# Two projected tiles of a Mamba-2 stage accumulate in another PSUM pool

## The chip, the cores and the metric

The kernel runs on 1 core of one Trainium2 chip. The metric is the device time of one launch in microseconds (us), the median of several runs. TensorE (PE) multiplies matrices into PSUM, VectorE (DVE), ScalarE (ACT) and GpSimd (POOL) work elementwise, and SyncE (SP) issues most of the DMAs. Each engine takes its instructions strictly in the order in which they were built and waits at the first one whose operands are not ready.

## The reference

One inference step of a two-layer trunk for 256 prompt tokens and 8 x 8 sample tokens, 320 columns together. Layer 0 mixes with a chunked gMLP, layer 1 with a Mamba-2 SSD block, and each is followed by a squared-ReLU MLP. The change is in the SSD block:

```python
def mamba2_mixer(h, ...):
    zxbcdt = h @ w_in                      # 1024 -> 2048 z, 4096 xbc, 32 dt
    xbc_c = silu(conv(xbc))                # causal, width 4
    dt = softplus(dt_raw + dt_bias)
    y, new_ssm = ssd_scan(xs, dt, -exp(a_log), bm, cm, ssm_state)
    y = (y + xs * d_skip) * silu(z)
    out = rms_norm(y by group, norm_g) @ w_out
```

Here `ssd_scan` needs the running sum of `dt * a` over the positions (`acum`), its exponentials, the products C B^T per group, and per head small products with the state. There are 8 groups of 4 heads.

## The kernel before

Activations lie transposed, features on the 128 partitions and the 320 columns in the free dimension. A weight matrix is read in tiles of 1024 x 128. Each is loaded by a DMA on SP's queue into `raw` (5 buffers), rounded on ACT to `whi` (L136) and its remainder taken on DVE as `wlo` (L137), with 3 buffers each (`NHI`). A tile then takes 8 x 3 matmuls of 128 x 320 (L307, L308, L309: `whi` with the high and the low part of the input, `wlo` with the high part), which accumulate in one PSUM bank.

PSUM has four pools. `psm` (names `mm`) has three banks and `psx` (names `ax`) three; `psa` (`adap`) and `psn` (`nrm`) have one each. Projected tiles take a bank of `mm`. The small products of the SSD work take banks of `ax`.

In the SSD stage the first five tiles (`w_dt` and `w_in` 0 to 3) are computed ahead of the norm. From index 4 on `in_tile` calls `proj_h`, one tile at a time. The order of the tiles, by their index i, is by groups of six: B, C, two of X, two of Z. Group 1 has i = 6 to 11, so i = 8 and 9 (the ninth and the tenth) are its two X tiles, and 10 and 11 its two Z tiles. B, C and X go through `conv` (L634): an evacuation by ACT into `cb` (three buffers, L640 and L641), a convolution of one ACT and three DVE instructions (L646, L649), and a SiLU (L651, L652). A Z tile is read by one ACT instruction (L815).

Beside the tiles runs a chain for `dt` (L820 to L860): a series on DVE (L829), the scan for `acum` (L836), exponentials on ACT (L838), the packing on POOL (L845 to L848), two stores to DRAM (L850, L851), and PE transposes of the packed rows (L854, L859). From the stored rows each group loads `bc` and `ea`, broadcast to all partitions (L673, L674); `bc` has two buffers. The convolutions after the first ones are held back behind the scan (L647).

`ssd` does one group's work in pieces (`yield`), which `convs` of the next group interleaves with its tiles: C B^T into `pc` (L681) and its masking to `cbm` on DVE (L683); the decay factors in `bc` by twelve ACT instructions (L687) and an exponential (L688); transposes (L697 to L717); state products (L735); `cp` (L745); the outputs (L757); the gating with Z (POOL L769), squares (ACT L774) and their mean (DVE L776, PE L210); the new state (L785 to L802).

The order on each engine isn't that of the code. The tile framework is opened with `schedule_with_timeline_sim=True`: it simulates the whole program with its own estimates of durations, and places each instruction on its engine, and each tile in a buffer of its pool, by that timeline. A change in one place can so move instructions on every engine behind it. `tc.issue_after` adds a constraint to that order.

Of the kernel before, what the change touches and what calls it, by code (L numbers as in the profile page):

```python
# [52 lines left out]
def tile_trunk(ctx: ExitStack, tc: tile.TileContext, io):  # L53
    nc = tc.nc
    pe, act, dve, pool = nc.tensor, nc.scalar, nc.vector, nc.gpsimd
# [12 lines left out]
    def nm(s):  # L68
        uid[0] += 1
        return f"{s}{uid[0]}"  # L70
# [30 lines left out]
    def mm_ps():  # L101
        return psm.tile([P, 512], F32, tag="mm", name=nm("mm"))

    def ax_ps():
        return psx.tile([P, 512], F32, tag="ax", name=nm("ax"))
# [34 lines left out]
    def wload(src, w=P, eng=dve):  # L140
        fill["n"] += fill["rate"]
        while fill["n"] >= 1:
            fill["n"] -= 1
            if fill["q"]:
                step()
        raw = raw_tile()
        nc.sync.dma_start(raw, src)
        return [t.rearrange("p (a b) -> p a b", b=w) for t in split(raw, eng=eng)]
# [156 lines left out]
    def mm3(ps, w, kk, hi, lo, first, last, n=T):  # L305
        whi, wlo = w
        pe.matmul(ps[:, :n], lhsT=whi[:, kk, :], rhs=hi, start=first, stop=False)  # L307
        pe.matmul(ps[:, :n], lhsT=whi[:, kk, :], rhs=lo, start=False, stop=False)  # L308
        pe.matmul(ps[:, :n], lhsT=wlo[:, kk, :], rhs=hi, start=False, stop=last)  # L309

    def proj1(srcs, hi, lo, eng=dve):
        ps = mm_ps()
        n = 8 * len(srcs)
        for kc, src in enumerate(srcs):
            w = wload(src, eng=eng)
            for kk in range(8):
                k = kc * 8 + kk
                mm3(ps, w, kk, hi(k), lo(k), k == 0, k == n - 1)
        return ps

    h_hi = lambda k: hhi[:, k, :]
    h_lo = lambda k: hlo[:, k, :]

    def proj_h(src, eng=dve):
        return proj1([src], h_hi, h_lo, eng)

    def proj_g(src, g, ps):
        ghi, glo, _ = g
# [5 lines left out]
    def scaled(ps, r):  # L334
        c = tp.tile([P, 10], F32, tag="sc", name=nm("sc"))
        act.copy(c, ps[:, T:G])
        t = scratch()
        dve.tensor_tensor(t, ps[:, :T], r, MUL)
        dve.tensor_tensor(b1(t[:, TP:]), b1(t[:, TP:]), bb(c[:, 1:9]), ADD)
        dve.tensor_scalar(t[:, :TP], t[:, :TP], c[:, 0:1], None, ADD)  # L340
        return t
# [5 lines left out]
    def mlp(l, gc, g, nxt):  # L347
        A, S = amul[2 * l + 1], mod(l, 3)
        r = rstd_x()
        c, mp = new_pool("left" if l else "right")  # L350
        mhi = mp.tile([P, NF, T], F32R, name=f"mhi{l}")
        mlo = mp.tile([P, NF, T], F32R, name=f"mlo{l}")

        def ev1(m, ps):
            t = scratch()
            act.activation(t, ps[:, :T], AF.Relu)  # L356
            s = scratch()
            pool.tensor_tensor(s, t, t, MUL)  # L358
            act.activation(mhi[:, m, :], s, AF.Copy)  # L359
            dve.tensor_tensor(mlo[:, m, :], s, mhi[:, m, :].bitcast(F32), SUB)  # L360

        pss = [proj_g(io["mlp_w1"][l, m], g, mm_ps() if m < 3 else ax_ps()) for m in range(MG)]
        gc.close()
        ev1(0, scaled(pss[0], r))
        norm(A, S, r)
        for m in range(1, MG):
            ev1(m, scaled(pss[m], r))
        for m in range(MG, NF):
            ev1(m, proj_h(io["mlp_w1"][l, m]))
        ng = nxt()  # L370
        gate = mod(l, 5)
        for m in range(KD):
            ps = proj1([io["mlp_w2"][l, m, kc] for kc in range(4)], lambda k: mhi[:, k, :], lambda k: mlo[:, k, :])
            residual(ps, m, gate, ng)
        c.close()
        return ng
# [191 lines left out]
    for m in range(16):  # L568
        ev_u(m, proj_h(io["gm_wu"][m]))
        while len(us) > 9:  # L570
            spatial(sp)
            sp += 1
# [9 lines left out]
    for m in range(KD):  # L582
        ps = proj1([io["gm_wo"][m, kc] for kc in range(2)], lambda k: uhi[:, k, :], lambda k: ulo[:, k, :])
        residual(ps, m, gate, g)
# [35 lines left out]
    ps = scaled(pss[0], r0)  # L620
# [6 lines left out]
    def in_tile():  # L627
        i = widx[0]
        widx[0] += 1
        if i < MG - 1:  # L630
            return scaled(pss[1 + i], r0)
        return proj_h(io["w_in"][i])

    def conv(ct, tag, bufs):  # L634
        ps = in_tile()
        cb = mb.tile([P, CW], F32, tag="cb", name=nm("cb"), bufs=3)
        cs = cb[:, 3 + TP :].rearrange("p (b t) -> p b t", t=11)
        pool.memset(cb[:, 0:3], 0.0)
        pool.tensor_copy(cs[:, :, 0:3], scv[:, ct])
        act.copy(cb[:, 3 : 3 + TP], ps[:, :TP])  # L640
        act.copy(cs[:, :, 3:], b1(ps[:, TP:T]))  # L641
        pool.tensor_copy(cvp[:, ct, :], cb[:, TP : TP + 3])
        pool.tensor_copy(scv[:, ct], cs[:, :, 8:])
        o = mb.tile([P, CW], F32, tag="co", name=nm("co"), bufs=3)
        wv = lambda k: vec[:, V_CW + ct * 4 + k : V_CW + ct * 4 + k + 1]
        act.activation(o[:, :CO], cb[:, :CO], AF.Identity, scale=wv(0), bias=vec[:, V_CB + ct : V_CB + ct + 1])  # L646
        with tc.issue_after(dtl[0]) if dtl else ExitStack():  # L647
            for k in range(1, 4):
                dve.scalar_tensor_tensor(o[:, :CO], cb[:, k : k + CO], wv(k), o[:, :CO], MUL, ADD)  # L649
        r = mb.tile([P, T], F32, tag=tag, name=nm(tag), bufs=bufs)  # L650
        act.activation(r[:, :TP], o[:, :TP], AF.Silu)  # L651
        act.activation(b1(r[:, TP:]), o[:, 3 + TP :].rearrange("p (b t) -> p b t", t=11)[:, :, 0:8], AF.Silu)  # L652
        return r
# [150 lines left out]
    def convs(g_, prev):  # L804
        B = conv(16 + g_, "Bt", 2)
        next(prev, None)
        C = conv(24 + g_, "Ct", 2)
        next(prev, None)
        X = []
        for r in range(2):  # L810
            X.append(conv(2 * g_ + r, "Xt", 4))
            next(prev, None)
        Z = mt([P, 2, T], "Z", 2)
        for r in range(2):
            act.activation(Z[:, r], in_tile()[:, :T], AF.Silu)  # L815
            next(prev, None)
        return B, C, X, Z
# [291 lines left out]
```

## Time and profile before

| | us |
|---|---|
| median of 3 runs | 1078.03 |
| lowest, highest | 1077.81, 1082.76 |
| the profiled execution | 1075.66 |
| its span, first to last instruction | 1073.9 |
| PE busy in the span | 1030.2 (96%) |
| DVE, ACT, POOL busy | 652.9, 549.2, 299.9 |

The span lies 1.8 us below the execution's own time, for what is ahead of the first instruction and behind the last. PE is busy nearly all the time, and its clock is granted at one of two levels, 1.2 or 2.4 GHz. In the page's row of clocks a 9 is (nearly) all of a slice at 2.4 GHz; the share over the span is 0.986. The SSD stage with its 48 projected tiles stands between about 500 and 760 us.

### The profile page before, as it was taken

Reading aid. Unit: us, or ns where it says so; the run is one execution under the profiler, and the core shown is the slowest. Engines: PE = TensorE matmul, PEld = TensorE weight load, DVE = VectorE, ACT = ScalarE, POOL = GpSimd, SP = SyncE. Lnnn points to the kernel's source line nnn. Section 1 sums busy time; section 2 is a strip of 40 time slices with the busy share of each in tenths; the row PEclk is TensorE's granted clock in tenths of the full one; section 3 lists DMA queues with packets and bytes.
Section 4 is the critical chain, followed back from the end, with each engine's and each line's share of the span. In section 5 each row is a group of like instructions: output and inputs, shape, how many; then the busy total and the mean of one; then the engine's idle time right before and its main releaser. Section 6 shows DMA issues by size and latency. Waiting matters only on the chain.

```text
span 1073.9 us, 19747 instructions
## 1 busy us (share of the span) xinstructions
PE 1030.2 (96%) x7809; PEld 970.8 (90%) x7809; DVE 652.9 (61%) x1080; ACT 549.2 (51%) x1013; POOL 299.9 (28%) x403
## 2 busy tenths in 40 slices
PE   5999999999999999999688999999999999999996
PEld 3778998999999999999688999999999999999995
DVE  4545966437644443446968898898876754444432
ACT  4453343435644433335698777678345555543331
POOL 1200134332433311222123333532217243411001
PEclk9999999999999999999888999999999999999998
DMA  9957985775666667455435656565445544544431
GB/s 366 361 194 237 335 316 166 267 253 195 243 215 216 217 223 271 151 157 172 151 108 171 251 168 222 197 224 205 167 163 158 177 157 140 155 153 144 155 99 50
DMA packets 60877, 213.97 MB, mean 199 GB/s; under 512 B 6560, under 2 KB 12128, under 8 KB 58480
## 3 DMA queue, kind: packets, MB, share of 16 engines
q1 hardware_dynamic: 58544, 200.47, 55.1%
q0 software_dynamic: 1952, 11.98, 3.1%
q8 instruction: 61, 1.00, 0.4%
q10 hardware_dynamic: 288, 0.26, 0.1%
q14 instruction: 32, 0.26, 0.1%
HBM read 199.31 MB, written 12.85 MB: 198 GB/s over the span
## 4 chain that ended last, share of the span: by engine, by line
PE 76%; ACT 7%; DVE 6%; issue 5%; DMA 3%; POOL 2%; SPq 0%; POOLq 0%; ACTq 0%; DVEq 0%
PE mm L307 19%; PE mm L308 19%; PE mm L309 19%; PE adap L165 3%; ACT bc L687 2%; DMA bc<-rowd 2%; DVE wlo L137 2%; DVE co L649 2%; ACT whi L136 1%; PE mm L411 1%; PE mm L412 1%; PE mm L413 1%; PE ax L757 1%; DMA raw<-ada 1%; PE ax L307 1%
## 5 line engine op out<-in xcount | busy, mean ns | idle before, releaser
L137 DVE TENSOR_TENSOR wlo<-raw,whi 128x1024 fp32r<-128x1024 f32 (+1 forms) x243 | 298.1, 1228 | 203.5 <-ACT whi L136 202.6
L136 ACT ACTIVATE whi<-raw 128x1024 fp32r<-128x1024 f32 (+1 forms) x243 | 254.7, 1050 | 252.4 <-PE mm L308 195.0
L307 PE MATMUL mm<-hhi,whi 128*128 128x320 f32 x952 | 300.1, 316 | 1.9 <-ACT ta L356 0.9
L308 PE MATMUL mm<-hlo,whi 128*128 128x320 f32 x952 | 296.8, 313 | 0.1
L309 PE MATMUL mm<-hhi,wlo 128*128 128x320 f32 x952 | 296.9, 313 | 0.0
L307 PEld LDWEIGHTS mm<-hhi,whi 128*128 128x128 f32 x952 | 180.2, 190 | 7.5 <-issue 3.3
L308 PEld LDWEIGHTS mm<-hlo,whi 128*128 128x128 f32 x952 | 180.1, 189 | 1.9 <-DVE hlo L267 1.0
L309 PEld LDWEIGHTS mm<-hhi,wlo 128*128 128x128 f32 x952 | 180.0, 189 | 1.4 <-DVE mv L198 0.4
L307 PE MATMUL mm<-mhi,whi 128*128 128x320 f32 x512 | 158.3, 309 | 0.0
L308 PE MATMUL mm<-mlo,whi 128*128 128x320 f32 x512 | 158.1, 309 | 0.0
L309 PE MATMUL mm<-mhi,wlo 128*128 128x320 f32 x512 | 158.0, 309 | 0.0
L358 POOL TENSOR_TENSOR ta<-ta 128x320 f32<-128x320 f32 x64 | 82.0, 1285 | 140.0 <-ACT ta L356 118.2
L307 PEld LDWEIGHTS mm<-mhi,whi 128*128 128x128 f32 x512 | 96.1, 188 | 1.2 <-issue 0.8
L308 PEld LDWEIGHTS mm<-mlo,whi 128*128 128x128 f32 x512 | 96.1, 188 | 0.0
L309 PEld LDWEIGHTS mm<-mhi,wlo 128*128 128x128 f32 x512 | 96.1, 188 | 0.0
L293 POOL TENSOR_TENSOR x<-x,rs 128x64 f32<-128x64 f32 x28 | 11.2, 399 | 218.5 <-DVE rs L292 218.5
L359 ACT ACTIVATE mhi<-ta 128x320 fp32r<-128x320 f32 x64 | 30.1, 471 | 81.9 <-POOL ta L358 81.6
L360 DVE TENSOR_TENSOR mlo<-ta,mhi 128x320 fp32r<-128x320 f32 x64 | 33.5, 523 | 59.2 <-ACT mhi L359 59.2
L649 DVE SCALAR_TENSOR_TENSOR co<-cb,vec,co 128x344 f32<-128x344 f32 x96 | 54.7, 585 | 6.1 <-ACT co L646 5.9
L165 PE MATMUL adap<-ara,sc 128*32 128x256 f32 x640 | 43.0, 383 | 0.0
L307 PE MATMUL mm<-uhi,whi 128*128 128x320 f32 x128 | 40.0, 315 | 0.0
L308 PE MATMUL mm<-ulo,whi 128*128 128x320 f32 x128 | 40.0, 315 | 0.0
(340 smaller groups left out, 1691.8 us busy)
## 6 DMA issues: line engine op xcount, KB each, us to landing
raw<-mlp_w SPq DMA_DIRECT2D x128, 512.0 KB, 3.6
ara<-ada_w SPq DMA_DIRECT2D x80, 512.0 KB, 6.3
raw<-w_in SPq DMA_DIRECT2D x48, 512.0 KB, 3.7
raw<-ada SPq DMA_DIRECT2D x16, 512.0 KB, 9.9
raw<-gm_wv SPq DMA_DIRECT2D x16, 512.0 KB, 8.7
raw<-gm_wu SPq DMA_DIRECT2D x16, 512.0 KB, 5.8
raw<-gm_wo SPq DMA_DIRECT2D x16, 512.0 KB, 5.3
st<-state SPq DMA_DIRECT2D x8, 1024.0 KB, 5.5
```

The source lines that it names most:

```text
L136: act.activation(hi[:, :n], raw[:, :n], AF.Copy)
L137: eng.tensor_tensor(lo[:, :n], raw[:, :n], hi[:, :n].bitcast(F32), SUB)
L165: pe.matmul(ps[32 * j : 32 * j + 32, :256], lhsT=sc[:, kb + i, :], rhs=rs[i][:, j * 256 : (j + 1) * 256], start=(kb + i == AB - 1), stop=( ...
L293: (dve if m == KD - 1 else pool).tensor_tensor(x[:, m, TP:], x[:, m, TP:], t0, ADD)
L307: pe.matmul(ps[:, :n], lhsT=whi[:, kk, :], rhs=hi, start=first, stop=False)
L308: pe.matmul(ps[:, :n], lhsT=whi[:, kk, :], rhs=lo, start=False, stop=False)
L309: pe.matmul(ps[:, :n], lhsT=wlo[:, kk, :], rhs=hi, start=False, stop=last)
L358: pool.tensor_tensor(s, t, t, MUL)
L359: act.activation(mhi[:, m, :], s, AF.Copy)
L360: dve.tensor_tensor(mlo[:, m, :], s, mhi[:, m, :].bitcast(F32), SUB)
L649: dve.scalar_tensor_tensor(o[:, :CO], cb[:, k : k + CO], wv(k), o[:, :CO], MUL, ADD)
L687: act.activation(bc[:, h, cq[c]], bc[:, h, cq[c]], AF.Relu, bias=nat[:, c, HG * g_ + h : HG * g_ + h + 1], scale=-1.0)
```

## The change

`proj1` and `proj_h` take an optional PSUM tile. `in_tile` passes a bank of `ax` for i = 8 and i = 9; all other tiles keep `mm`.

```diff
-    def proj1(srcs, hi, lo, eng=dve):
-        ps = mm_ps()
+    def proj1(srcs, hi, lo, eng=dve, ps=None):
+        ps = ps or mm_ps()
...
-    def proj_h(src, eng=dve):
-        return proj1([src], h_hi, h_lo, eng)
+    def proj_h(src, eng=dve, ps=None):
+        return proj1([src], h_hi, h_lo, eng, ps)
...
         if i < MG - 1:
             return scaled(pss[1 + i], r0)
-        return proj_h(io["w_in"][i])
+        return proj_h(io["w_in"][i], ps=ax_ps() if i in (8, 9) else None)
```

No instruction is added or removed in the computation. The order changes on all engines from about 521 us on. In the rows below the tiles' accumulators are, by i: `mm870` 7, `mm883` or `ax883` 8, `mm897` or `ax897` 9, `mm909` 10, `mm916` 11, `mm931` 12; `whi` and `wlo` with numbers near theirs are their weights.

PE at the head of the stage, before: tile 8 ends, then come the packed rows' transposes, group 0's first products, and tile 9.

```order
L309 MATMUL mm883_5629<-hhi_81,wlo886_5633 128x320
L854 MATMUL ax823_5329<-cst_78,yst1_5250 128x128 x3
L859 MATMUL ax825_5336<-cst_78,dup0824_5334 128x128 x2
L697 MATMUL adap880_5619<-cst_78,Bt833_5364 128x128 x2
L681 MATMUL ax868_5547<-Ct838_5385,Bt833_5364 128x128 x2
L681 MATMUL ax868_5547<-Ct838_5385,Bt833_5364 128x64
L307 MATMUL mm897_5698<-hhi_81,whi899_5701 128x320
```

PE at the same place of the changed kernel:

```order
L309 MATMUL mm916_5842<-hhi_81,wlo919_5846 128x320
L854 MATMUL ax823_5329<-cst_78,yst1_5250 128x128 x3
L859 MATMUL ax825_5336<-cst_78,dup0824_5334 128x128 x2
L697 MATMUL adap880_5619<-cst_78,Bt833_5364 128x128 x2
L681 MATMUL ax868_5547<-Ct838_5385,Bt833_5364 128x128 x2
L681 MATMUL ax868_5547<-Ct838_5385,Bt833_5364 128x64
L307 MATMUL mm931_5923<-hhi_81,whi933_5926 128x320
L308 MATMUL mm931_5923<-hlo_82,whi933_5926 128x320
L307 MATMUL ax883_5629<-hhi_81,whi885_5632 128x320
```

Tiles 10 and 11 have moved ahead of the transposes, and tile 8 behind them and behind the first two matmuls of tile 12. Tiles 8 and 9 are given the same bank of `ax`, the one that `pc` (`ax868`) holds before; tiles 10 and 11 share one bank of `mm`, while tiles 6 and 7 hold the other two.

DVE shortly behind that place, the difference (- before, + now): the masking of `pc`, the product `cp` that needs the loaded `ea`, and convolutions.

```order
 L649 SCALAR_TENSOR_TENSOR co842_5401<-cb841_5394,vec_79,co842_5401 128x344
-L683 TENSOR_TENSOR cbm869_5551<-ax868_5547,cst_78 128x320
 L745 TENSOR_TENSOR cp907_5753<-ea828_5343,Ct838_5385 128x768
 L649 SCALAR_TENSOR_TENSOR co847_5422<-cb846_5415,vec_79,co847_5422 128x344
 L649 SCALAR_TENSOR_TENSOR co866_5539<-cb865_5532,vec_79,co866_5539 128x344
 L649 SCALAR_TENSOR_TENSOR co847_5422<-cb846_5415,vec_79,co847_5422 128x344
+L683 TENSOR_TENSOR cbm869_5551<-ax868_5547,cst_78 128x320
```

The masking, which frees the bank of `pc`, has moved behind `cp` and three convolution steps.

ACT some 160 us later, while tile 35 is projected and group 4's output is finished: the squares (L774) of group 4 and the decay factors (L687) on the `bc` that is loaded for group 6.

```order
 L613 COPY dup21229_7727<-Xt1183_7429 128x256
-L774 ACTIVATE Z1118_7021<-Y1193_7476 128x640
 L687 ACTIVATE bc1209_7607<-bc1209_7607,nat_5087 128x128 x2
 L687 ACTIVATE bc1209_7607<-bc1209_7607,nat_5087 128x64
 L687 ACTIVATE bc1209_7607<-bc1209_7607,nat_5087 128x128 x2
 L687 ACTIVATE bc1209_7607<-bc1209_7607,nat_5087 128x64
-L687 ACTIVATE bc1209_7607<-bc1209_7607,nat_5087 128x128
-L136 ACTIVATE whi1235_7742<-raw1234_7740 128x1024
-L687 ACTIVATE bc1209_7607<-bc1209_7607,nat_5087 128x128
-L815 ACTIVATE Z1188_7443<-mm1196_7530 128x320
+L687 ACTIVATE bc1209_7607<-bc1209_7607,nat_5087 128x128 x2
+L774 ACTIVATE Z1118_7021<-Y1193_7476 128x640
```

The squares have moved from ahead of the first decay factors to behind eight of the twelve. On PE there, the mean (L210 into `nrm1201`) stood behind 24 matmuls of tile 35 and 19 of tile 36 after the outputs of group 4; now it stands behind 20 and 11.

## Rows read from the trace of the kernel before

**Rows 1.** The page: span, granted clock by slice, and the weight remainders' group.

```profile
span 1073.9 us, 19747 instructions
...
PEclk9999999999999999999888999999999999999998
...
L137 DVE TENSOR_TENSOR wlo<-raw,whi 128x1024 fp32r<-128x1024 f32 (+1 forms) x243 | 298.1, 1228 | 203.5 <-ACT whi L136 202.6
```

**Rows 2.** PE's waits: line and releaser, us in total, times, longest.

```profile
PE ax L854 <- POOL yst L847: 8.1, 1, 8.1
PE ax L794 <- DVE xst L729: 2.9, 1, 2.9
...
PE ax L735 <- ACT Bn L701: 1.8, 1, 1.8
...
PE adap L713 <- DVE Bst L704: 1.3, 2, 1.0
...
PE nrm L210 <- DVE ta L776: 0.6, 1, 0.6
```

**Rows 3.** Three stretches: PE, PEld, DVE, ACT, POOL busy (instructions), granted clock, DMA.

```profile
531.27:544.92 13.65, 7.50 (x29) 6.70 (x30) 10.20 (x19) 9.85 (x32) 5.22 (x16) 0.50 0.63 199
544.92:568.82 23.90, 19.25 (x203) 18.45 (x203) 15.99 (x26) 23.79 (x53) 4.26 (x18) 1.00 0.29 93
568.82:575.64 6.82, 6.82 (x25) 5.71 (x23) 6.82 (x6) 6.24 (x19) 3.54 (x2) 0.50 0.48 148
```

**Rows 4.** PE in order of time at the stage's head: start, us, [idle before <-releaser].

```profile
520.59 0.31 PE L307 MATMUL mm<-hhi,whi 128*128 128x320 f32 x1
...
522.24 0.31 PE L307 MATMUL mm<-hhi,whi 128*128 128x320 f32 x1
...
524.00 0.31 PE L307 MATMUL mm<-hhi,whi 128*128 128x320 f32 x1
...
536.37 0.90 PE L854 MATMUL ax<-cst,yst 128*128 128x128 f32 x3 [8.10 <-POOL yst L847]
...
540.75 0.61 PE L307 MATMUL mm<-hhi,whi 128*128 128x320 f32 x1
...
546.01 0.38 PE L699 MATMUL adap<-cst,dup 128*128 128x128 f32 x2
```

**Rows 5.** ACT, then DVE, in order of time at the same place.

```profile
524.93 1.06 ACT L136 ACTIVATE whi<-raw 128x1024 fp32r<-128x1024 f32 x1 [1.63 <-PE mm L308]
...
524.48 2.07 DVE L829 SCALAR_TENSOR_TENSOR yst<-yst 128x320 f32<-128x320 f32 x4
...
532.22 0.95 DVE L836 TENSOR_TENSOR_SCAN yst<-cst,yst 128x320 f32<-128x320 f32 x1
...
542.50 0.96 DVE L745 TENSOR_TENSOR cp<-ea,Ct 128x768 f32<-128x768 f32 x1 [0.99 <-DMA ea<-rowd]
543.38 3.01 DVE L649 SCALAR_TENSOR_TENSOR co<-cb,vec,co 128x344 f32<-128x344 f32 x6
```

**Rows 6.** PE, SP, ACT and DVE in order of time behind group 4's outputs.

```profile
687.39 0.41 PE L307 MATMUL mm<-hhi,whi 128*128 128x320 f32 x1
...
688.86 0.38 SPq L673 DMA_DIRECT2D bc<-rowd  x1
...
693.86 0.74 ACT L774 ACTIVATE Z<-Y 128x640 f32<-128x640 f32 x1 [5.55 <-POOL Y L769]
...
694.64 0.49 DVE L776 TENSOR_TENSOR ta<-Z 128x320 f32<-128x320 f32 x1 [2.23 <-ACT Z L774]
...
695.05 2.05 ACT L687 ACTIVATE bc<-bc,nat 128x128 f32<-128x128 f32 x7 [0.45 <-DMA bc<-rowd]
...
695.18 0.83 PE L210 MATMUL nrm<-ones_g,ta 128*128 128x1 f32 x6 [0.58 <-DVE ta L776]
```

**Rows 7.** The loads of `bc` (line 673): who waited (us, times), and landing.

```profile
  ACT bc L687: 15.0, 5
...
DMA to landing us min/median/max: 4.1/5.2/6.5
```

## Prediction

> **What bounds the kernel now.** I read the page first: PE fills the span but for small gaps, and the granted clock sags in three slices at the SSD stage and in the last one [rows 1]. So time can be won or lost only as idle time of PE or as time at 1.2 GHz. PE's waits, read next, name one big idle, 8.1 us at the transposes of the packed `dt` rows (L854), and behind it 2.9 us at the new state (L794) and 1.8 us at L735; the rest of the stage has waits of about 1 us and less [rows 2]. The busy time by stretch then shows what the clock adds: 1.2 GHz from 531.27 to 544.92, behind the first idle, and again for 6.82 us from 568.82, right behind the wait at L794, while between them it was full; 0.50 in that view is 1.2 GHz and 1.00 is 2.4 [rows 3]. All three views point at the head of the stage, which is where the change begins; the timelines of PE, ACT and DVE there show why [rows 4, 5]. PE stops at 528.27 (536.37 less 8.10) because the two accumulators of group 1's B and C tiles cannot be emptied until group 0's convolutions go on, and those are held behind the scan, which starts at 532.22.
>
> A matmul of a tile costs 0.147 us at 2.4 GHz: 12 of them from 522.24 to 524.00 [rows 4], so a tile of 24 costs 3.53. At 1.2 GHz it is about 0.27: 25 in 6.82 us [rows 3]. A stretch of 6.82 us at the low clock therefore loses 6.82 x (1 - 0.147/0.27) = 3.1 us.
>
> The profiled execution took 1075.66 us, its span and 1.8 us around it; the median of the three runs is 2.37 us higher. I work out the difference against the profiled execution and put it on the median of 1078.03.
>
> **The change part by part.** No instruction is added or taken away, so the sum is one of waits. I take three places.
>
> *First place, 520 to 546 us.* The two tiles that leave `mm` let tiles 10 and 11 (Z, whose accumulator one SiLU empties without the held convolution) run ahead of L854. That is one tile more, 3.53 us of work, in front of the wait of 8.10. But these two do not run freely.
>
> Tile 7 starts at 520.59 and ends by 24 x 0.147 at 524.1. The weights of tiles 8 and 9 are already cast and keep two of the three `whi` buffers until those tiles run, now behind L854. So the cast for tile 10 waits for tile 7's last use of the third, and takes 1.06 [rows 5]: tile 10 starts at about 525.3. Its third matmul needs `wlo`, which stands on DVE behind three steps of the series (four take 2.07) and takes 1.23 [rows 1, 5]: about 527.2. With 22 x 0.147 it ends at 530.5. The same third buffer serves tile 11: cast until 531.6, then the SiLU of tile 10 must empty their common bank, and tile 11 starts at about 531.9. Its `wlo` stands on DVE behind the scan and three convolution steps of 0.50 [rows 5]: one remainder fewer than before stands ahead of the scan, so this ends at 532.2 + 0.95 - 1.2 + 1.5 = 533.5, and the remainder at 534.7. Then 22 matmuls at 0.147 or 0.27: tile 11 ends, and L854 starts, between 538.0 and 540.7. Before, it started at 536.37.
>
> Behind L854, tile 8 waits for the bank of `pc`, that is for `cbm`, and on DVE `cbm` now stands behind `cp`, which waits for the `ea` load. That load hangs on ACT's exponential of the scan. The scan is earlier, but ACT has the SiLU of tile 10 and a table load ahead of the exponential, so I leave the arrival at 542.50 as it is [rows 5]. `cp` 0.96, three steps of 0.50 and `cbm` 0.49: tile 8 starts at about 545.5, with 2 matmuls of tile 12 done. Before, tile 9 started at 540.75 and by 546.01 had 21 of its 24 matmuls [rows 4]. At 546 the old order so has tiles 7, 8 and 21 matmuls; the new one has 7, 10, 11 and 2 to 5 matmuls of 12 and 8, 5 to 8 ahead, 0.7 to 1.2 us. Whether the clock stays low a little longer is open by about 2 us. I take 0 for this place, from -2 to +2. The idle of 8.10 isn't removed; it is cut into waits for casts, for one bank and for a mask.
>
> *Second place, 546 to 687 us.* Group 0's outputs (L757) stood behind 2 matmuls of tile 13 and now stand behind all of it and 2 each of tiles 14 and 15. Two tiles of cover come in front of L735 and L794, so their 1.8 and 2.9 go, and with them probably the low clock behind L794: 1.8 + 2.9 + 3.1 = 7.8 us won at most. What is late next: the groups' chains run two tiles later against the projections for groups 0 and 1, one for group 2. The `bc` loads, which wait for the outputs of two groups before, come later by as much, and five of the eight hold ACT up already, 15.0 us in all [rows 7]; casts stand behind them. Tiles 13, 14 and 15 start in turn with two matmuls each, and each needs a cast and a remainder of 1.06 + 1.23 in which PE has 0.3 us of work: 2 us or so are lost there. At L713, which waits for `Bst` on DVE, the longest wait was 1.0; two remainders stand near it now, so 1 to 2.5 us in one group. A few waits of the 1 us kind follow from the shift, and one more stretch of low clock (3.1) is as likely as not. That is 5 to 10 us against 7.8. I take 0, from -6 to +4.
>
> *Third place, 687 to 702 us.* Times are from the first matmul behind group 4's outputs, 687.39. Before, PE reached L210 at 695.18 - 0.58 = 694.60, after 43 matmuls and eight of L794: 7.21 us. Now 31 stand ahead: 7.21 - 12 x 0.147 = 5.45. The release came at 7.79. From PE's order alone the wait grows from 0.58 to 2.34. But ACT's squares now stand behind eight decay factors on a `bc` that is still in flight: issued at 688.86, in use at 695.05, which is 7.66. Eight of L687 at 2.05 / 7 = 0.29 give 10.0, the squares 0.74, DVE's sum 0.49 and the two hand-overs 0.1: 11.3. The wait is then 11.3 - 5.45 = 5.9, 5.3 more than before. `bc` took 6.1 here; with the shortest and the longest of the eight loads (4.1 and 6.5) [rows 6, 7] the growth is 3.3 and 5.7. Both idles of 2.9 us and more in this stage were followed by the low clock and those of 1.8 and less were not [rows 2, 3], so I add 3.1, with 0 as the other end. Together +8.4, from +3.3 to +8.8.
>
> The Trainium skill speaks against this change in the same direction ("TensorE: Matmul & The Clock Gate", section "HAM oscillation — how this bites in real kernels"): a stream of matmuls that is cut again and again by waits falls back to the half clock each time and pays for the way back each time, so several middling waits can cost more than one long one. The trace agrees where it can, with the 3.1 us behind a wait of only 2.9. By that rule the sum is the one taken here; without it, it is 3.1 less.
>
> Sum: 0 + 0 + 8.4 = +8.4, which I round to +8. On the profiled execution that is 1083.7, on the median **1086**.
>
> **The rivals.**
>
> *The wait at L854 goes and nothing takes its place (faster).* One tile more runs in front of it, and the low clock behind it is shorter. For it: 8.10 idle and 13.65 us at low clock are the largest loss in the span. Against it: only 3.53 us of work is added, and the casts of both tiles are chained through one buffer. Worth at most 3.5 of idle, 2 of clock at the head, and the 7.8 of the second place; less 4 at a mild third place that is 9: 1078 - 9 = 1069. It decides if casts and masks come about 2 us earlier than I have them.
>
> *The new order loses as much as it wins (no change).* If `bc` lands in 4.1 us at the third place and the clock holds there, it costs 3.3, and 2 to 3 won at the second place cancel it: 1078 to 1080. For it: the loads' spread of 4.1 to 6.5. Against it: the order on ACT is fixed, so some of the 5 us is lost in every case.
>
> *More places like the third (slower still).* The same order, decay factors ahead of other work, can hold ACT in other groups, and each wait near 3 us can bring 3.1 of low clock. With two more, +14: 1092. For it: the 15.0 us that ACT waits for `bc` already. Against it: by group 4 the outputs stand at nearly their old place again, so the shift dies out.
>
> *The tiles do not get another bank of use.* Tile 8 in `ax` waits for `pc`, and the pool gives no spare bank; in effect the change only swaps the Z tiles with the X tiles. This is already in the sum.
>
> **How the numbers follow.** Forecast, +8 with its own range of 1081 to 1090: 0.56. Slower still: 0.18. No change: 0.18. Faster: 0.08. About 0.5%, 5.4 us, is what a measurement of this kernel can tell from no change: 1072.6 to 1083.4. Of the forecast's case a small part lies below 1083.4, about as much as of the no-change case lies above. So faster 0.08, same 0.18, slower 0.74. The range 1078 to 1093 leaves out the faster case, the low half of no change and the far end of the slower one.
>
> **What would show it.** In the profile after, PE's wait at L854 should be gone or under 1 us, with waits of 1 to 2 us at L307 and L309 for `whi` and `wlo` just ahead of it, and one of about 2 us at the start of the tile in `ax`, released by DVE L683. The waits at L794 and L735 near 552 and 568 should be gone. A wait of 4 to 6 us at L210 released by DVE L776, some 10 us later in the span than before, should be the largest of the stage, with the clock at 1.2 GHz behind it. If L210's wait stays under 2 us, or the kernel comes out under 1075, the third place is wrong; if PE idles nowhere and the time is still longer, the whole sum is.

## The result and the profile after

The changed kernel took 1089.76 us (median of 20 runs, 1084.11 to 1096.18), the kernel before 1078.78 in the same rounds (20 runs, 1075.36 to 1084.54): a ratio of **1.0095, with a 95% interval of 1.0077 to 1.0113**. The change makes the kernel slower by about 1%. The profiled execution of the changed kernel took 1084.21 us, 8.55 more than that of before, and it is one of the quickest of its runs; what follows explains these 8.55 us, and of the other 2.4 by which the medians differ only the runs' times speak.

The page after, its span and the granted clock by slice (before: [rows 1]):

```profile
span 1082.4 us, 19739 instructions
...
PEclk9999999999999999999999999899999999999998
```

The page counts 8 instructions fewer than before; PE, DVE and POOL compute with as many as before, and ACT has two loads of its function tables (ACT_TABLE_LOAD) less. The three slices of 8 at the head of the SSD stage (some 510 to 590 us) are gone. One slice of 8 has come far behind them, from 676 to 704 us: it is the third place. PE's waits from 500 us on (line and releaser, us in total, times, longest; before: [rows 2]):

```profile
PE nrm L210 <- DVE ta L776: 6.0, 2, 4.9
PE mm L307 <- ACT whi L136: 4.5, 4, 1.8
PE mm L307 <- ACT Z L815: 4.2, 2, 2.9
PE mm L309 <- DVE wlo L137: 3.7, 2, 2.4
...
PE ax L307 <- DVE cbm L683: 1.1, 1, 1.1
...
PE adap L713 <- DVE Bst L704: 0.3, 1, 0.3
```

The waits of 8.1 at L854, 1.8 at L735 and 2.9 at L794 are gone (of L794 a wait of 0.2 is left, with another releaser). In their place stand casts (`whi`, `wlo`), a SiLU (`Z`, L815), a mask (`cbm`), and 4.9 us at L210. To see where each is, the head first, PE in order of time (start, us, idle before and its releaser; before: [rows 4]):

```profile
525.94 0.42 PE L307 MATMUL mm<-hhi,whi 128*128 128x320 f32 x1 [1.00 <-ACT whi L136]
...
527.87 0.41 PE L309 MATMUL mm<-hhi,wlo 128*128 128x320 f32 x1 [1.38 <-DVE wlo L137]
...
532.69 0.41 PE L307 MATMUL mm<-hhi,whi 128*128 128x320 f32 x1 [1.33 <-ACT Z L815]
...
535.60 0.42 PE L309 MATMUL mm<-hhi,wlo 128*128 128x320 f32 x1 [2.35 <-DVE wlo L137]
...
540.47 0.49 PE L854 MATMUL ax<-cst,yst 128*128 128x128 f32 x3
...
543.78 0.42 PE L307 MATMUL mm<-hhi,whi 128*128 128x320 f32 x1 [1.77 <-ACT whi L136]
...
545.42 0.41 PE L307 MATMUL ax<-hhi,whi 128*128 128x320 f32 x1 [1.08 <-DVE cbm L683]
```

L854 follows its neighbour without a gap, at 540.47 instead of 536.37: a tile more lies in front of it, and so do four waits of 6.06 us together. Then the third place, in rows of PE, SP, ACT and DVE (before: [rows 6]):

```profile
686.90 0.41 PE L308 MATMUL mm<-hlo,whi 128*128 128x320 f32 x1
...
687.98 0.38 SPq L673 DMA_DIRECT2D bc<-rowd  x1
...
693.71 2.33 ACT L687 ACTIVATE bc<-bc,nat 128x128 f32<-128x128 f32 x8 [6.28 <-DMA bc<-rowd]
695.96 0.72 ACT L774 ACTIVATE Z<-Y 128x640 f32<-128x640 f32 x1
...
696.71 0.49 DVE L776 TENSOR_TENSOR ta<-Z 128x320 f32<-128x320 f32 x1 [5.19 <-ACT Z L774]
...
697.25 1.44 PE L210 MATMUL nrm<-ones_g,ta 128*128 128x1 f32 x6 [4.91 <-DVE ta L776]
```

ACT stands idle for 6.28 us on a `bc` in flight, with the squares (L774) queued behind the eight decay factors that wait for it. Before, the squares came first, and the wait for `bc` was behind them.

A fourth place, which the prediction doesn't have, is seen in rows of ACT, POOL and PE some 70 us later:

```profile
762.88 0.74 ACT L774 ACTIVATE Z<-Y 128x640 f32<-128x640 f32 x1 [5.36 <-POOL Y L769]
...
764.24 1.04 ACT L136 ACTIVATE whi<-raw 128x1024 fp32r<-128x1024 f32 x1
765.19 0.41 ACT L815 ACTIVATE Z<-mm 128x320 f32<-128x320 f32 x1
...
756.43 6.42 POOL L769 TENSOR_TENSOR Y<-Y,Z 128x640 f32<-128x640 f32 x1 [3.85 <-DVE Y L768]
...
765.65 0.64 PE L307 MATMUL mm<-hhi,whi 128*128 128x320 f32 x1 [2.87 <-ACT Z L815]
```

Here it is the squares that stand in front. They wait 5.36 us for POOL's gate (L769); behind them wait a cast and the SiLU that empties a bank of `mm`, and PE waits 2.87 us for that bank. In the kernel before, the SiLU stood in front (ACT and POOL):

```profile
755.99 0.42 ACT L815 ACTIVATE Z<-mm 128x320 f32<-128x320 f32 x1
760.41 0.74 ACT L774 ACTIVATE Z<-Y 128x640 f32<-128x640 f32 x1 [3.65 <-POOL Y L769]
...
754.36 6.02 POOL L769 TENSOR_TENSOR Y<-Y,Z 128x640 f32<-128x640 f32 x1 [3.87 <-DVE Y L768]
```

The gate was long there too, 6.02 us against 6.42, and PE had no wait at this place.

The clock at these places, by stretch (PE, PEld, DVE, ACT, POOL busy with instructions, granted clock, DMA; before: [rows 3]):

```profile
536.60:540.00 3.40, 3.40 (x15) 3.40 (x15) 2.64 (x5) 3.02 (x8) 1.61 (x9) 0.51 0.92 315
...
560.50:563.90 3.40, 3.40 (x12) 3.01 (x13) 3.40 (x4) 3.38 (x7) 2.07 (x3) 0.50 0.39 118
...
635.60:639.00 3.40, 3.40 (x16) 3.36 (x15) 1.45 (x2) 3.37 (x6) 1.33 (x3) 0.50 0.76 306
...
697.10:703.90 6.80, 6.64 (x27) 6.65 (x28) 4.83 (x13) 6.18 (x11) 0.90 (x3) 0.50 0.45 148
...
765.30:768.70 3.40, 3.05 (x11) 3.05 (x12) 3.40 (x6) 0.66 (x2) 0.58 (x1) 0.50 0.00 0
```

Within the SSD stage the time at 1.2 GHz is the same as before, 20.4 us against 13.65 + 6.82 = 20.5. But before, PE was idle for 6 of them and worked for 14.3; now it works for 19.9.

**Where the 8.55 us are.** For every profile I set PE's time against its work, each matmul at the mean time that its kind takes at 2.4 GHz, and read off how much later than the kernel before it reaches the same amount of work. The growth of that lag between points of before's clock, in us (experiments first, to be used below):

| profile of | up to 500 | 500 to 687 | 687 to 702 | 702 to 740 | 740 to 800 | 500 to 800 |
|---|---|---|---|---|---|---|
| after | +0.6 | -1.8 | **+7.4** | -2.5 | **+4.7** | +7.8 |
| e1 squares first, group 6 | +3.8 | +3.0 | +4.7 | -2.7 | +5.7 | +10.7 |
| e2 tile 8 alone | +2.3 | +1.8 | +4.5 | +2.3 | +3.6 | +12.2 |
| e3 tile 9 alone | +3.2 | -0.6 | +3.6 | -2.3 | +6.2 | +6.9 |
| e4 three bc buffers | +7.4 | +5.4 | 0.0 | -0.7 | -1.5 | +3.2 |
| e5 squares first, all groups | +4.1 | +1.6 | +3.3 | -2.3 | +5.4 | +8.0 |
| e6 nrm bank, three bc | +1.5 | -1.3 | -0.8 | -1.5 | +2.5 | -1.1 |
| e7 before, three bc | +4.3 | +3.9 | -0.8 | -1.5 | +0.4 | +2.0 |
| e8 tile 9 alone, three bc | +5.4 | +4.3 | -0.2 | -2.5 | +4.2 | +5.8 |
| e9 SiLU first | +1.2 | -0.7 | +6.8 | -2.8 | +0.2 | +3.5 |
| e10 both orders | +0.9 | +1.4 | +4.7 | -2.8 | +0.2 | +3.5 |
| e11 e8 and SiLU first | +5.3 | +3.9 | -0.3 | -0.4 | +1.2 | +4.4 |

Nothing in the order of the instructions differs in the first column, so its 0.6 to 7.4 us are what one execution differs from another by (the experiments ran on three chips); two columns of different profiles are compared by places, and whole kernels by the ratios alone.

### The profile page after: what moved, and what is told of

The parts are those of the page before. It is cut to its first block, busy times and chain, and to the rows that moved or that the text cites. A ratio compares the mean times of both kernels' runs of the same rounds, so it can differ in the third digit from the quotient of the medians.

```text
span 1082.4 us, 19739 instructions
## 1 busy us (share of the span) xinstructions
PE 1034.4 (96%) x7809; PEld 974.4 (90%) x7809; DVE 655.2 (61%) x1080; ACT 547.2 (51%) x1011; POOL 304.9 (28%) x403
## 4 chain that ended last, share of the span: by engine, by line
PE 76%; DVE 6%; ACT 6%; DMA 5%; issue 5%; POOL 2%; SPq 0%; POOLq 0%; ACTq 0%; DVEq 0%
PE mm L307 19%; PE mm L308 19%; PE mm L309 19%; PE adap L165 3%; DMA bc<-rowd 2%; ACT bc L687 2%; DVE wlo L137 2%; PE ax L757 2%; DVE co L649 1%; PE mm L411 1%; PE mm L412 1%; PE mm L413 1%; ACT whi L136 1%; DMA raw<-ada 1%; PE ax L309 1%
## 5 line engine op out<-in xcount | busy, mean ns | idle before, releaser
L307 PE MATMUL mm<-hhi,whi 128*128 128x320 f32 x936 | 296.4, 317 | 10.4 <-ACT whi L136 4.5
L309 PE MATMUL mm<-hhi,wlo 128*128 128x320 f32 x936 | 293.4, 314 | 4.8 <-DVE wlo L137 4.8
L309 PEld LDWEIGHTS mm<-hhi,wlo 128*128 128x128 f32 x936 | 178.3, 191 | 6.8 <-DVE wlo L137 6.0
L309 PE MATMUL mm<-mhi,wlo 128*128 128x320 f32 x512 | 158.0, 309 | 0.0
L309 PEld LDWEIGHTS mm<-mhi,wlo 128*128 128x128 f32 x512 | 96.1, 188 | 0.0
L687 ACT ACTIVATE bc<-bc,nat 128x128 f32<-128x128 f32 (+1 forms) x96 | 27.9, 372 | 26.6 <-DMA bc<-rowd 26.6
L769 POOL TENSOR_TENSOR Y<-Y,Z 128x640 f32<-128x640 f32 x8 | 33.8, 4222 | 22.2 <-DVE Y L768 22.2
```

Of the source, the lines that this page charges most:

```text
L687: act.activation(bc[:, h, cq[c]], bc[:, h, cq[c]], AF.Relu, bias=nat[:, c, HG * g_ + h : HG * g_ + h + 1], scale=-1.0)
L769: pool.tensor_tensor(Y, Y, Z, MUL)
```

## The experiments

Each ran in five rounds together with the kernel before, and its ratio is against the runs of before in the same rounds. Theory A says that the loss is ScalarE's order: at a few places its queue stands on something late while the work PE needs is behind it. Theory B says that it is the head's new waits and the clock. What either means for an experiment stands in its expectation, and differs from one to the next.

**e1: the decay factors of one group held behind the squares.** The constraint applies to group 6 alone, whose factors had overtaken at the third place.

```diff
-        for h in range(HG):
-            for c in range(3):
+        with tc.issue_after(sqs[g_ - 2]) if g_ in (6,) else ExitStack():
+            for h, c in [(h, c) for h in range(HG) for c in range(3)]:
...
-        act.activation(q0, Y, AF.Square)
+        sqs[g_] = act.activation(q0, Y, AF.Square).ins
```

> The changed kernel, with one constraint more: group 6's decay factors (L687) are issued on ACT only behind group 4's squares (L774). All engines keep their order up to about 690 us. Theory A (the order on ACT makes the third place): L210's wait of 4.9 us behind DVE L776 falls to about 2.3, which PE's earlier arrival alone leaves, the low clock behind it goes, and the kernel is 3 to 6 us faster than the changed one, +0.4 to +0.7% against before. Theory B (the wait is late data whatever ACT's order, because the whole chain of the groups is late): L210 still waits 4 us or more and the time stays within 2 us of the changed kernel, +0.8 to +1.0%.

Measured 1.0053 (1.0030 to 1.0077), 0.42% less than the change. PE's row at the third place:

```profile
702.05 1.44 PE L210 MATMUL nrm<-ones_g,ta 128*128 128x1 f32 x6 [2.64 <-DVE ta L776]
```

The wait is 2.64 instead of 4.91. Counted from the first matmul behind group 4's outputs (694.70 in this trace), L210 is released at 7.35 us; it was 10.35 in the change (697.25 - 686.90) and 7.79 before. So with the squares in front nothing comes late any more. What is left is that PE comes early: 34 matmuls stand there in front of L210, against 39 in the change and 51 before, so the constraint has moved five more behind it. The clock still falls behind the wait of 2.64, which A did not expect. The ratio is in A's range, but this undoes a part, not all.

**e2 and e3: one tile alone in `ax`.**

```diff
-        return proj_h(io["w_in"][i], ps=ax_ps() if i in (8, 9) else None)
+        return proj_h(io["w_in"][i], ps=ax_ps() if i == 8 else None)   # e2; i == 9 in e3
```

> Only tile 8 takes a bank of ax; tile 9 stays in mm. Group 4's squares then stand behind four decay factors on a bc in flight and group 5's behind nine; tile 10 is not ahead of L854, whose wait stays 7 to 8 us. Theory A: waits of about 3 us at L210 in these two groups, time +0.3 to +0.7% against before. Theory B (the bank at the head is what costs): the Z tiles do not move, so no loss at the head and a time within 0.2% of before.

> Only tile 9 takes a bank of ax; tile 8 stays in mm. Group 4's squares stand ahead of the decay factors as before, group 3's behind ten and group 5's behind seven. L854's wait stays 7 to 8 us. Theory A: the loss depends on the order that comes out, and here little is left in front at group 4: L210's waits 2 us or less each, time 0 to +0.3%. Theory B (a projected tile in ax holds up the small products whichever it is): as much as tile 8 alone, half of the whole change or more, +0.5% or more.

Measured 1.0092 (1.0073 to 1.0111) and 1.0089 (1.0058 to 1.0120): each alone costs as much as both. For e2 neither theory had that. For e3 it is in B's numbers, but B's cause isn't in the trace: of the `ax` banks e3's PE waits have the 8.1 us at L854, as before the change, and one of 0.2. PE's waits, of e2 and then of e3:

```profile
PE nrm L210 <- DVE ta L776: 6.1, 3, 3.4
```

```profile
PE mm L307 <- ACT Z L815: 3.1, 2, 2.9
PE nrm L210 <- DVE ta L776: 2.6, 1, 2.6
```

Both keep the whole wait of 8.1 us at L854, the line of before [rows 2], so a loss of this size doesn't need the changed kernel's head with its cut-up waits. The kind of the third place is there in both, in e2 at three groups. The fourth place is in e3 alone; e2 has no wait there, and what it loses behind 740 us (+3.6) goes with 6.8 us at 1.2 GHz from 794.5 us on, ahead of which PE had no wait of 0.3 us or more for 27 us. I had weighed the tiles one by one; but what differs between the three arrangements is the order that follows, and each of them brings a bad one.

**e4: three buffers for `bc`.** One line on top of the change.

```diff
-        return yp.tile(shape, dtype, tag=tag, name=nm(tag), bufs=2)
+        return yp.tile(shape, dtype, tag=tag, name=nm(tag), bufs=3 if tag == "bc" else 2)
```

> The changed kernel with three buffers for bc in place of two, so that each group's bc can be loaded a group earlier. The head up to about 546 us is the same. Theory A: bc has landed when ACT comes to its decay factors, ACT's waits for it (15 us in the kernel before) go to under 5, L210's wait to under 1.5, and the time falls to within 0.4% of the kernel before on either side. Theory B: the head and the shift of the groups cost the same, and the time stays at +0.7% or more.

Measured 0.9985 (0.9963 to 1.0008): the whole 1% is back, with both tiles in `ax` and, up to 560 us, the order of the changed kernel. So the head's cut-up waits are not the loss, unless the buffer gains as much elsewhere, which e7 tests. ACT and PE at the third place:

```profile
706.81 0.74 ACT L774 ACTIVATE Z<-Y 128x640 f32<-128x640 f32 x1 [5.54 <-POOL Y L769]
708.47 2.05 ACT L687 ACTIVATE bc<-bc,nat 128x128 f32<-128x128 f32 x7 [0.92 <-DMA bc<-rowd]
...
708.13 0.83 PE L210 MATMUL nrm<-ones_g,ta 128*128 128x1 f32 x6 [0.59 <-DVE ta L776]
```

These are nearly the rows of before [rows 6]: the squares stand in front, L210 waits 0.59, and the lag at that place is 0.0. PE's order is that of before too, with 51 matmuls in front of L210. The load itself still comes just after the squares; what the third buffer changed is the order, on all engines from about 560 us on. At the fourth place, ACT and POOL:

```profile
768.45 0.74 ACT L774 ACTIVATE Z<-Y 128x640 f32<-128x640 f32 x1 [2.52 <-POOL Y L769]
770.76 0.42 ACT L815 ACTIVATE Z<-mm 128x320 f32<-128x320 f32 x1
...
764.88 3.53 POOL L769 TENSOR_TENSOR Y<-Y,Z 128x640 f32<-128x640 f32 x1 [3.35 <-DVE Y L768]
```

Here the squares are still in front of the SiLU, as in the change. But the gate takes 3.53 us instead of 6.42, and PE does not wait. This profile is the slowest of its kernel's 12 runs (1086.51, median 1078.72), so its other columns say little.

**e7: the control, three buffers in the kernel before.** The same line without the change.

> The kernel before (both tiles in the mm banks) with three buffers instead of two for the rows bc. Theory A, by which the third buffer repaired only what the change had done to ScalarE's order: the kernel before waits 15.0 us at L687 for rows on their way, but its L210 waits behind L776 are short (0.58 us at the third place), so little of it reaches TensorE: ratio to before 0.996 to 1.002, some 1074 to 1083 us. Theory B, by which the third buffer is a gain of its own of about 1 % that merely offsets the change, and the change's loss is still all there: ratio 0.987 to 0.993, some 1068 to 1073 us.

Measured 1.0002 (0.9985 to 1.0019). ACT's wait for `bc` in total, times, longest, which was 15.0, 5 [rows 7]:

```profile
ACT bc L687 <- DMA bc<-rowd: 9.5, 2, 5.7
```

ACT waits 5.5 us less and the time is the same: B's way out, that the third buffer is a gain of its own, is closed. It isn't a plain repair either. In the kernel before, too, it brings another order, on ACT from 561 us on, with a wait of 2.46 us at an L210 that has 39 matmuls in front (at 638.81). What the two runs show is that the order it brings costs nothing on balance, with the change or without it.

**e5: the constraint of e1 at all groups.** The one difference from e1 is `if g_ in range(2, NG)` in place of `if g_ in (6,)`.

> The changed kernel with every group's decay factors (L687) held in ScalarE's order behind the squares (L774) of the group two earlier, at all of groups 2 to 7 and not only at group 6. Theory A, by which the squares' place in ScalarE's order is the loss at the third place and a place like it at 760 to 800 us the rest: ratio to before 0.997 to 1.004, against 1.0095 for the change and 1.0053 with the order of one group alone. Theory B, by which the loss comes from the waits for casts at the head (L307 and L309 at 525 to 547 us) and from TensorE's clock: no better than the order of one group, ratio 1.004 to 1.010. A third outcome: holding rows back everywhere delays the decay matmuls L713 and costs more than the squares gain, ratio above 1.010.

Measured 1.0088 (1.0059 to 1.0116), in B's numbers: no gain that can be told from the change itself. Theory A in this form fell: "squares first, everywhere" is no cure. (B's cause, the head, is ruled out by e4.) The third place is better by 4 us in the table, but the fourth, where the squares are already in front, is as bad as in the change (+5.4), and PE's waits have the same line for L815 as after the change, 4.2, 2, 2.9. That holds for e1 nearly as much (+5.7), so the table doesn't show why e1 is quicker than e5; the two intervals overlap, and one profile of each can't settle it.

**e6: other banks.** Tile 8 in the bank of the mean squares (`nrm`), tile 9 in `mm` as before, three buffers for `bc`.

```diff
-        return proj_h(io["w_in"][i], ps=ax_ps() if i in (8, 9) else None)
+        return proj_h(io["w_in"][i], ps=nrm_ps() if i == 8 else None)
...
-        return yp.tile(shape, dtype, tag=tag, name=nm(tag), bufs=2)
+        return yp.tile(shape, dtype, tag=tag, name=nm(tag), bufs=3 if tag == "bc" else 2)
```

> Three buffers for bc, and other banks for the two tiles: tile 8 (ninth counted from 0) in a bank of the nrm pool, tile 9 in the mm pool as in the kernel before. Theory A (waits decide by bank and by ScalarE's order): the ninth tile doesn't wait for a bank of ax, the wait of 8.1 us at L854 stays or is cut as in the change, no bank of ax is held by a projection in the stage's head, and with the rows in time the time falls a little below before: ratio 0.992 to 1.000. Theory B (a projected tile outside mm costs something wherever it goes, by the waits for casts): ratio 1.003 to 1.010.

Measured 0.9983 (0.9964 to 1.0001), 1077.13 us. It is 1.1% quicker than the changed kernel, in A's numbers, and can't be told from the one before. Nor can it be told from e4, so the third buffer alone may have done it. PE's waits at the head:

```profile
PE ax L854 <- POOL yst L847: 5.8, 1, 5.8
PE mm L307 <- ACT cb L641: 4.9, 2, 3.9
```

8.1 became 5.8 at L854 and 3.9 stands a little later for a bank of `mm`, which a held convolution empties. A bank more doesn't bring the head forward; it moves the wait.

**e8: tile 9 alone, with three buffers.** This is e3 with the line of e4.

> Three buffers for bc, and tile 9 alone in a bank of ax, tile 8 in mm. Tile 9 alone without the third buffer gave 1.0089. Theory A: with the rows in time its loss goes as that of both tiles did (1.0095 to 0.9985): ratio 0.994 to 1.000. Theory B, by which the loss of tile 9 alone lies in the order of the casts and in the wait for Z at L815, which the third buffer doesn't touch: ratio 1.003 to 1.009.

Measured 1.0030 (1.0009 to 1.0050), at the edge of B's numbers: the third buffer takes 0.6 of e3's 0.9%. The third place is gone in the table (-0.2), the fourth is not (+4.2): PE's waits have e3's line for L815 unchanged, 3.1, 2, 2.9. ACT and PE at the third place:

```profile
702.19 2.05 ACT L687 ACTIVATE bc<-bc,nat 128x128 f32<-128x128 f32 x7 [6.05 <-PE ax L794]
704.15 0.72 ACT L774 ACTIVATE Z<-Y 128x640 f32<-128x640 f32 x1
...
708.14 0.72 PE L210 MATMUL nrm<-ones_g,ta 128*128 128x1 f32 x6
```

The squares stand behind seven decay factors again, and PE doesn't wait all the same: here 68 matmuls stand in front of L210, against 39 in the change. So late squares on ACT cost PE nothing where enough work stands in front of L210. The two places are two losses, and the next three runs take the second by itself.

**e9: the SiLU first, at the fourth place.** The squares of group 6 go behind the SiLU that empties the bank, as they did in the kernel before.

```diff
-        act.activation(q0, Y, AF.Square)
+        with tc.issue_after(zs[7]) if g_ == 6 else ExitStack(): act.activation(q0, Y, AF.Square)
...
-            act.activation(Z[:, r], in_tile()[:, :T], AF.Silu)
+            zs[g_] = act.activation(Z[:, r], in_tile()[:, :T], AF.Silu).ins
```

> The changed kernel, with the squares L774 of group 6 held in ScalarE's order behind the SiLU L815 that empties the bank that PE waits for at 765.6 us. Theory A (the fourth place, 760 to 800 us, is a loss of its own, made by that order): the wait of 2.9 us for Z at L815 goes and with it the 1.2 GHz behind it, so 3 to 5 us less than the change: ratio to before 1.004 to 1.007 against 1.0095. Theory B (the fourth place only shows a delay that was made at the third, and would come out somewhere else): no gain, ratio 1.008 to 1.011.

Measured 1.0045 (1.0027 to 1.0063), 0.5% less than the change. ACT and POOL there:

```profile
760.02 0.42 ACT L815 ACTIVATE Z<-mm 128x320 f32<-128x320 f32 x1
764.46 0.74 ACT L774 ACTIVATE Z<-Y 128x640 f32<-128x640 f32 x1 [4.03 <-POOL Y L769]
...
757.19 7.23 POOL L769 TENSOR_TENSOR Y<-Y,Z 128x640 f32<-128x640 f32 x1 [3.85 <-DVE Y L768]
```

POOL's gate is even longer, 7.23 us, ACT waits 4.03 for it, and PE doesn't notice: the wait of 2.87 and the 1.2 GHz behind it are gone (+0.2 in the table instead of +4.7). Ahead of 760 us this kernel has ACT's and DVE's order of the change. So the fourth place is a loss of its own, and it is the order, not the length of the gate alone, that lets it reach PE. The gate counts too: in e2, e4 and e6 the squares stand in front as in the change, the gate takes 3.53 or 3.54 us, and PE has no wait for the bank there. In after, e1, e3, e5 and e8 it takes 6.40 to 6.42, and PE waits there 1.3 to 2.9 us.

**e10: both orders.** The constraints of e1 and of e9 together.

> The changed kernel with both orders of ScalarE repaired: the decay factors of group 6 behind the squares of group 4 (which alone gave 1.0053), and the squares of group 6 behind the SiLU L815. Theory A, by which these two places are the whole loss: ratio to before 0.998 to 1.003. Theory B, by which the head's waits for casts or the clock hold a part of it: 1.004 to 1.008.

Measured 1.0027 (1.0010 to 1.0045), in A's numbers. The two orders give back 0.7 of the 0.95%, less than the sum of 0.42 and 0.50, though within what the intervals allow. What is left has a row that would account for it, PE at the third place:

```profile
697.20 1.44 PE L210 MATMUL nrm<-ones_g,ta 128*128 128x1 f32 x6 [2.54 <-DVE ta L776]
```

That is PE's own order again: 34 matmuls stand in front of L210, as in e1, against 51 before, and 6.8 us at 1.2 GHz follow. The constraint on ACT doesn't bring them back. In e4, where 51 stand there, the wait is 0.59. No run takes this rest by itself.

**e11: e8 with the SiLU first.**

> Tile 9 alone in ax and three buffers for bc (which gave 1.0030, with the wait of 2.9 us for Z at L815 left in its trace), and the squares L774 of group 6 behind that SiLU. Theory A, by which that wait is what is left of its loss: ratio to before 0.997 to 1.001. Theory B, by which the rest lies elsewhere: no change from 1.003, that is 1.001 to 1.005.

Measured 1.0004 (0.9986 to 1.0022), in A's numbers: with the fourth place taken as well, nothing is left of the loss that can be told. For one tile as for two there are two places. Here the first went with e8's order on PE and the second with the SiLU in front. In this profile, the slowest of its 12 runs, the gate is short as well (3.54), so that e9 is the better witness for the order.

## Why the prediction came out right, and where it didn't

The forecast was 1086 with 1078 to 1093, slower; measured 1089.76. The sum of +8.4 stands against +8.55 between the two profiled executions, but its parts don't match as well as that.

**First place: right.** Tile 10 was to start at 525.3, its third matmul at 527.2, tile 11 at 531.9, its `wlo` at 534.7, L854 between 538.0 and 540.7, tile 8 at 545.5. The trace has 525.94, 527.87, 532.69, 535.60, 540.47 and 545.42. That one idle would be "cut into waits for casts, for one bank and for a mask" is the list of waits after, row by row. The wait for the mask was 1.08 where about 2 was expected. And the cause that the prediction gives for PE's stop at 528.27, two accumulators that cannot be emptied, is a guess at why the scheduler chose that order; what PE waited for there by the trace is L854's packed rows from POOL [rows 2].

**Second place: right in sum.** The waits at L735 and L794 are gone and small ones have come; the one at L713 did not grow (0.3). First and second place together are -1.8 where 0 was forecast.

**Third place: right in mechanism, a little too large.** PE reached L210 at 5.44 us behind the outputs (697.25 - 4.91 - 686.90), forecast 5.45. The factors began at 6.81 instead of 7.66, since `bc` was issued 0.39 us sooner (1.08 behind that point, not 1.47) and was in use 5.73 after its issue, not 6.19; that is why the wait is 4.91 and not 5.9. Growth of the wait, 4.91 - 0.58 = 4.3, and 3.1 for the 6.8 us of low clock make the 7.4 of the table; forecast 8.4. Of the 4.3, PE's earlier arrival makes 7.21 - 5.44 = 1.8 and the later release 10.35 - 7.79 = 2.6; e1 and e10, with releases at 7.35 and 7.25, show that the second part is ACT's order. The wait came 2 us later in the span than before, not "some 10".

**Not foreseen: the fourth place, +4.7.** Of it 2.87 is idle and 3.4 x (1 - 0.147 / 0.27) = 1.5 is for the 3.4 us at 1.2 GHz. The rival "more places like the third" has its kind but not its content: it had decay factors ahead of other work; here the squares are ahead. The step that missed it is the choice of three places, up to 702 us. It was hidden in the sum because 1.8 + 2.5 us were won elsewhere. So the total came out so close partly by cancelling, which is luck.

**The clock.** The trace after doesn't keep to the rule read from before, that waits of 2.9 and more bring the low clock and those of 1.8 and less don't: two waits of 1.03 and 0.70 within 1.3 us stand ahead of the stretch at 560.5, one of 1.08 at L210 ahead of that at 635.6, and in e2 none at all ahead of that at 794.5. What I cite the Trainium skill for ("TensorE: Matmul & The Clock Gate", section "HAM oscillation — how this bites in real kernels"), that a stream cut by waits pays for the way back each time, agrees with the trace in the number of stretches, five short ones in place of two. The time at 1.2 GHz did not grow, it is 20 us in both. Dearer is the 5.6 us more of PE's work inside it, worth 5.6 x 0.46 = 2.6.

**What stays open.** The median grew by 2.4 us more than the profiled execution did. The 0.27% that e10 leaves was not isolated. And why the scheduler takes squares or factors first in a given arrangement was not tried; the runs only show what either order costs.

## What to carry to other kernels

Moving an accumulator to another pool adds no work, but where a scheduler sets the order by its own timeline it can reorder every queue behind it; look at what stands in front of what on the engine that feeds the bottleneck, first of all where an instruction waits for a DMA or for a slow engine. A wait costs by what is queued behind it and by how much work the bottleneck still has in front: a gate of 6 to 7 us was free with the SiLU in front (before, e9) and cost 4.7 us with it behind, and late squares were free where 68 matmuls stood in front of the ones that need them (e8). Where a loss comes from such an order, a constraint at the one place can give it back, and so can a buffer more, by bringing another order. The same constraint everywhere gave no gain that could be told.

## What was not expected of the hardware

The gate L769 on POOL has one shape, and takes 3.52 to 7.23 us over all profiles. Whether it is long or short goes with DVE's work beside it. DVE in the changed kernel, where L769 ran 6.42 us from 756.43, then DVE and POOL in e6:

```profile
756.26 2.28 DVE L785 TENSOR_TENSOR st<-st,ea 128x2048 f32<-128x2048 f32 x1
758.47 0.95 DVE L745 TENSOR_TENSOR cp<-ea,Ct 128x768 f32<-128x768 f32 x1
759.33 2.09 DVE L874 TENSOR_TENSOR hlo<-yst,hhi 128x320 fp32r<-128x320 f32 x5
```

```profile
749.68 2.28 DVE L785 TENSOR_TENSOR st<-st,ea 128x2048 f32<-128x2048 f32 x1
751.89 2.32 DVE L745 TENSOR_TENSOR cp<-ea,Ct 128x768 f32<-128x768 f32 x1
...
749.85 3.54 POOL L769 TENSOR_TENSOR Y<-Y,Z 128x640 f32<-128x640 f32 x1 [2.39 <-DVE Y L768]
```

Both times L785 begins 0.17 us before the gate. In the first, L745 takes 0.95 us and the gate 2.9 longer; in the second L745 takes 2.32 and the gate is short. All 13 profiles keep to this: with an L745 of 2.3 us beside it the gate takes about 3.5, with one of 0.95 that begins 2.0 us behind its start about 4.4, and the nine gates of 5.6 us and more have L874 behind the short L745. One of the two engines pays, and it isn't the same one in every profile: e8 has the long form at this place (6.42) and e11 the short one (3.54), with the same order of instructions up to there. What decides it wasn't tested, and at the fourth place it is part of the loss.

And in the first 500 us, where every kernel has the same order, profiles differ by up to 7.4 us. In e4 the largest wait there at L309 for a remainder is 3.0 us, in the changed kernel 1.1, in the kernel before there is none of 1 us; a gain of a few us can't be read from the spans of two profiles.
